# Block mask of an attention kernel: 16 more contraction rows in kept key and query buffers in place of 128 small mask products

## Chip, cores and metric

The kernel runs on one core of one Trainium2 chip. The metric is the device time of one execution in microseconds (us): the median of three runs, and beside it one execution taken by the hardware profiler, whose trace all rows below come from.

## The reference, cut to what matters

The program is one step of a two-layer streaming encoder: layer 0 has latent attention and a state-space branch side by side, layer 1 is a convolution module. Only the attention of the 2048 prompt tokens is touched here:

```
def attend(q_n, q_r, k_n, k_r, v, mask):
    s = (einsum('bqhd,bkhd->bhqk', q_n, k_n)
         + einsum('bqhr,bkr->bhqk', q_r, k_r)) * ATTN_SCALE
    s = where(mask, s, -1e30)            # key_chunk <= query_chunk, CHUNK = 64
    return einsum('bhqk,bkhd->bqhd', softmax(s), v)
```

There are 8 heads; a query or key has 64 + 32 = 96 numbers, a value 64. Queries are taken in 16 blocks of 128. Since a chunk is 64 tokens, a block needs all keys up to its own end, except that its first 64 queries must not see its last 64 keys. That corner of 64 by 64 in the last 64 key columns of each block is all that the mask does here.

## The kernel before

The program has four stages: input projections and the state-space branch (phase a), the latent attention's projections, sample attention and gating (phase b), the prompt's attention (phase c), output projection and convolution layer (phase d). All matrix products are done on pairs of a high and a low part (`h`, `l`), with three products for one: high by high, low by high, high by low.

Phase c, which the change edits, works head by head and, in a head, block by block. For block b it computes 128 by 128(b+1) scores in pieces of up to 512 keys (`chunk`): three products L1302, L1303 and L1304 over 96 rows add up in one PSUM tile `s_ps`. The last piece of a block gets a fourth product, L1306: the stationary operand `mq` is one row of 128 (64 ones, 64 zeros, bf16), the moving one `mk` one row of 64 values of -1e30, so that it adds -1e30 to the masked corner. That is 8 x 16 = 128 such products. VectorE then copies the piece to SBUF and takes the row's maximum (L1307), ScalarE does the exponential (L1318), GpSimd multiplies by the reciprocal sum (L1326), TensorE transposes (L1345), ScalarE and VectorE split the transposed piece into high and low (L1354, L1355), and TensorE multiplies by the values (L1365, L1366). `fin` adds up, gates and stores (L1374 to L1386).

The order in which these pieces are issued is written by hand: every piece gets a due time (`cum`, `LEAD`, `spread`) and the pieces are sorted by it; the tile framework then orders the instructions of each engine with a simulated timeline, so that an instruction may move ahead of others where its inputs and memory are ready. Each engine runs its own instructions in order.

`load(h)` makes new tiles `kl`, `kh`, `ql`, `qh` and `v` for a head in one of two pools, `c_kx` for even heads and `c_k` for odd ones, and issues the transfers into `kl`, `ql` and `v` (L1274 to L1278). `halves` makes the high part and leaves the low part in place: for head 0 on ScalarE and VectorE (L1286, L1287), for the others on GpSimd (L1289, L1290). A new tile takes the memory of the tile of that name two heads ago, and its first writer waits until that one has been read for the last time. `c_kx` opens at the end of phase b, whose last steps are the query rotation on GpSimd (L483 to L486), the transposes L691 and L701, the copies L692 and L702, and the reciprocal roots that begin at L671.

Of the kernel before, what the change touches and what calls it, by code (L numbers as in the profile page):

```python
# [11 lines left out]
F32R = mybir.dt.float32r  # L12
BF = mybir.dt.bfloat16
I32 = mybir.dt.int32
AF = mybir.ActivationFunctionType
OP = mybir.AluOpType
# [3 lines left out]
TP = 2048  # L20
# [16 lines left out]
def f(ap):  # L37
    return ap.bitcast(F32)
# [22 lines left out]
class K:  # L61
# [1176 lines left out]
    def phase_c(self):  # L1238
        nc, A, S = self.nc, self.A, self.S
        with ExitStack() as es:  # L1240
            cp = self.pool(es, "c_c", 1)
            sp = self.pool(es, "c_s", 2)
            kps = (self.kx, self.pool(es, "c_k", 1))
            po = self.pool(es, "c_po", 2, PSUM)
            pt = self.pool(es, "c_pt", 3, PSUM)
            ps = self.pool(es, "c_ps", 3, PSUM)
            mq = cp.tile([1, 128], BF, name="mq")
            nc.vector.memset(mq, 0.0)
            nc.vector.memset(mq[:, :64], 1.0)
            mk = cp.tile([1, 64], BF, name="mk")  # L1250
            nc.vector.memset(mk, -1e30)
            hd = {}
            cnt = [0]
            FQ, FQL = 0, 3
            PF = 0
# [4 lines left out]
            CHN = ((0, 1024, (0, 8)), (1024, 1024, (8, 16)))  # L1260

            def load(h):
                t = {}
                kp = kps[h % 2]
                for nm in "hl":
                    t["k" + nm] = kp.tile([96, TP], F32R, name="k" + nm)
                    t["q" + nm] = kp.tile([96, TP], F32R, name="q" + nm)
                t["v"] = kp.tile([128, 16, 128], F32R, name="v")
                hd[h] = t
                for c0, n, vs in CH0 if h == 0 else CH1 if h == 1 else CHN:  # L1270
                    cc = slice(c0, c0 + n)
                    dma = (nc.scalar if c0 < AQ and h == 0 else nc.sync).dma_start
                    k, q = t["kl"], t["ql"]
                    dma(f(k[:64, cc]), S["kT"][h, :, cc])  # L1274
                    dma(f(k[64:, cc]), S["krT"][:, cc])
                    dma(f(q[:, cc]), S["qT"][h, :, cc])
                    if vs:
                        dma(f(t["v"][:, vs[0]:vs[1]]), S["v"][h, :, vs[0]:vs[1]])  # L1278
                    if h == 0:
                        for nm in "kq":  # L1280
                            halves(h, nm, c0, True)

            def halves(h, nm, c0, first=False):
                hi, lo = (hd[h][nm + s][:, c0:c0 + 512] for s in "hl")
                if first:
                    nc.scalar.activation(hi, f(lo), AF.Copy)  # L1286
                    nc.vector.tensor_tensor(lo, f(lo), f(hi), op=OP.subtract)  # L1287
                else:
                    nc.gpsimd.tensor_scalar(hi, f(lo), 1.0, 1.0, op0=OP.mult, op1=OP.mult)  # L1289
                    nc.gpsimd.tensor_tensor(lo, f(lo), f(hi), op=OP.subtract)  # L1290

            def scores(h, b):
                t = hd[h]
                nk = 128 * (b + 1)
                sb = sp.tile([128, TP if nk > 1024 else 1024], F32, name="s_sb" if nk > 1024 else "s_sm", bufs=4)
                st = sp.tile([128, 16], F32, name="s_st", bufs=6)
                q = slice(b * 128, b * 128 + 128)
                items = []

                def chunk(i, k0, n, last):  # L1300
                    o = ps.tile([128, 512], F32, name="s_ps")
                    nc.tensor.matmul(o[:, :n], t["qh"][:, q], t["kh"][:, k0:k0 + n], start=True, stop=False)  # L1302
                    nc.tensor.matmul(o[:, :n], t["ql"][:, q], t["kh"][:, k0:k0 + n], start=False, stop=False)  # L1303
                    nc.tensor.matmul(o[:, :n], t["qh"][:, q], t["kl"][:, k0:k0 + n], start=False, stop=not last)  # L1304
                    if last:
                        nc.tensor.matmul(o[:, n - 64:n], mq, mk, start=False, stop=True)  # L1306
                    nc.vector.tensor_scalar(sb[:, k0:k0 + n], o[:, :n], 1.0, st[:, i - 1:i] if i else None,  # L1307
                                            op0=OP.mult, op1=OP.max, accum_out=st[:, i:i + 1])
                    if last:
                        nc.vector.tensor_scalar(st[:, 5:6], st[:, i:i + 1], -ATT, None, op0=OP.mult)  # L1310
                        e0 = 0
                        parts = []
                        while e0 < nk:
                            m = nk - e0
                            m = m if m <= 1024 else 1024 if m > 1152 else 640
                            j = 8 + len(parts)
                            parts.append(j)
                            nc.scalar.activation(sb[:, e0:e0 + m], sb[:, e0:e0 + m], AF.Exp, bias=st[:, 5:6], scale=ATT, accum_out=st[:, j:j + 1])  # L1318
                            e0 += m
                        if len(parts) == 2:  # L1320
                            nc.vector.tensor_tensor(st[:, 8:9], st[:, 8:9], st[:, 9:10], op=OP.add)
                        nc.vector.reciprocal(st[:, 7:8], st[:, 8:9])  # L1322
                        e0 = 0
                        while e0 < nk:
                            m = min(1024, nk - e0)
                            nc.gpsimd.tensor_scalar(sb[:, e0:e0 + m], sb[:, e0:e0 + m], st[:, 7:8], 1.0, op0=OP.mult, op1=OP.mult)  # L1326
                            e0 += m

                k0, i = 0, 0
                while k0 < nk:  # L1330
                    n = nk - k0
                    if n > 512:
                        n = 384 if n == 640 else 512
                    items.append((0.42 * n / 512 * 1.55, lambda i=i, k0=k0, n=n, l=k0 + n == nk: chunk(i, k0, n, l)))
                    k0 += n
                    i += 1
                return sb, items
# [116 lines left out]
            for n, (h, a, b) in enumerate(steps):  # L1454
                t0, t1 = cum[n], cum[n + 1]
                if n % 16 == 0:
                    add(cum[max(0, n - 14)] - LEAD - 4 if n else -1e9, lambda h=h: load(h))
                    if n:
                        spread(cum[n - 9] - LEAD, cum[n - 2] - LEAD, 8, lambda i, h=h: halves(h, "kq"[i % 2], 512 * (i // 2)))
                spread(t0 - LEAD - (t1 - t0), t0 - LEAD, nchunks(b), sub(("S", n), mk_s(n)))  # L1460
                spread(t0, t1, (b + 4) // 4, sub(("T", n), mk_t(n)))
                if b % 2 == 1:
                    spread(t1 + AVD, t1 + AVD + (t1 - cum[n - 1]), 2 * a + 2, sub(("A", n), mk_a(n, (n // 2) % 2, None)))
# [568 lines left out]
```

## Time and profile before

| | us |
|---|---|
| median of 3 runs | 2432.97 |
| lowest and highest of them | 2428.14, 2435.06 |
| profiled execution | 2423.48 |
| its span, first to last instruction | 2421.7 |

| engine | busy us | share of the span |
|---|---|---|
| PE (TensorE matmul) | 2251.3 | 93% |
| PEld (TensorE weight load) | 2009.7 | 83% |
| DVE (VectorE) | 1833.4 | 76% |
| ACT (ScalarE) | 1180.1 | 49% |
| POOL (GpSimd) | 1419.9 | 59% |

The weight loads overlap the matmuls; the ends of matmuls are modelled, so that two matmuls in a row overlap in the listing and the distance from one start to the next is the better measure of what one costs. The shares are averages over four stages with different limits. Attention runs from about 886 us, the first score product, to about 1407 us.

### The profile page before, as it was taken

The numbers are of one execution on the slowest core, as the hardware profiler recorded it, in microseconds if no ns is written. First come the engines' busy times: TensorE is split into PE (matmuls) and PEld (weight loads), VectorE is DVE, ScalarE is ACT, GpSimd is POOL, SyncE is SP. The second block draws the span as 40 slices with busy tenths as digits, with TensorE's granted clock in tenths as the row PEclk, the third lists the DMA queues.
The fourth block names the chain that finished last, engine by engine and source line by source line (L and its number), as shares of the span: only waits on it lengthen the run. The fifth ranks groups of instructions, "written<-read, shape, count | busy, mean of one in ns | idle before, by whom it ended". The sixth has DMA issues, their size and how long they took to land. (4 is left out here: it accounts for less than half of the span.)

```text
span 2421.7 us, 39276 instructions
## 1 busy us (share of the span) xinstructions
PE 2251.3 (93%) x13599; PEld 2009.7 (83%) x13599; DVE 1833.4 (76%) x3998; ACT 1180.1 (49%) x2226; POOL 1419.9 (59%) x1320
## 2 busy tenths in 40 slices
PE   6788989999889979999999989999999999989996
PEld 6788989996558868888888888988888889989996
DVE  7763246975447658888887855999998999999984
ACT  4343356236436657767677744433333533533423
POOL 5232543216266566667777534686768888976861
PEclk9899999999999979999999999999999999999998
DMA  9887574315727772222222356755355246434452
GB/s 190 192 228 164 136 179 146 95 49 177 235 82 221 249 235 49 61 56 67 70 71 68 96 175 217 241 179 177 105 176 173 92 131 213 148 127 138 154 166 90
DMA packets 289671, 352.10 MB, mean 145 GB/s; under 512 B 79936, under 2 KB 231808, under 8 KB 288960
## 3 DMA queue, kind: packets, MB, share of 16 engines
q1 hardware_dynamic: 288768, 348.40, 48.9%
q8 instruction: 108, 1.77, 0.3%
q10 hardware_dynamic: 704, 1.18, 0.2%
q14 instruction: 91, 0.75, 0.1%
HBM read 255.72 MB, written 93.52 MB: 144 GB/s over the span
## 5 line engine op out<-in xcount | busy, mean ns | idle before, releaser
L1655 DVE SCALAR_TENSOR_TENSOR acc<-vt,cw,acc 128x384 f32<-128x384 f32 (+2 forms) x1142 | 669.7, 659 | 2.4 <-ACT acc L1641 1.1
L1851 POOL TENSOR_TENSOR wl<-wr,wh 128x1024 fp32r<-128x1024 f32 x110 | 265.7, 2416 | 113.1 <-ACT wh L1850 111.8
L1850 ACT ACTIVATE wh<-wr 128x1024 fp32r<-128x1024 f32 x136 | 144.2, 1060 | 332.5 <-PE pp L72 173.9
L1355 DVE TENSOR_TENSOR ptl<-pt,pth 128x512 fp32r<-128x512 f32 (+2 forms) x320 | 186.1, 602 | 34.2 <-ACT pth L1354 32.9
L1354 ACT ACTIVATE pth<-pt 128x512 fp32r<-128x512 f32 (+2 forms) x320 | 161.5, 528 | 96.1 <-PE pt L1345 93.8
L71 PE MATMUL pp<-b0h,wh 128*128 128x512 f32 (+1 forms) x488 | 180.9, 371 | 6.6 <-ACT b0h L1758 6.0
L72 PE MATMUL pp<-b0l,wh 128*128 128x512 f32 (+1 forms) x488 | 180.8, 370 | 0.0
L1326 POOL TENSOR_SCALAR s_sb<-s_sb,s_st 128x1024 f32<-128x1024 f32 (+7 forms) x128 | 118.4, 938 | 105.5 <-DVE s_st L1322 47.3
L73 PE MATMUL pp<-b0h,wl 128*128 128x512 f32 (+1 forms) x488 | 180.1, 369 | 0.0
L1851 POOL TENSOR_TENSOR w<-wr,w 128x1024 fp32r<-128x1024 f32 x57 | 137.5, 2412 | 67.2 <-ACT w L1850 66.5
L71 PE MATMUL pp<-xh,vh 128*128 128x256 f32 (+1 forms) x448 | 133.8, 299 | 32.7 <-ACT vh L192 12.1
L1850 ACT ACTIVATE w<-wr 128x1024 fp32r<-128x1024 f32 x64 | 67.8, 1060 | 184.6 <-PE pp L72 113.5
L1366 PE MATMUL o<-ptl,v 128*128 128x256 f32 x576 | 151.8, 300 | 0.4 <-DVE ptl L1355 0.4
L1365 PE MATMUL o<-pth,v 128*128 128x256 f32 x576 | 149.8, 285 | 0.8 <-ACT pth L1354 0.8
L1302 PE MATMUL s_ps<-kh,qh 96*128 96x512 f32 (+3 forms) x320 | 131.8, 413 | 11.0 <-DVE s_sm L1307 6.9
L1345 PE MATMUL pt<-ident,s_sb 128*128 128x128 f32 x800 | 122.7, 279 | 12.4 <-POOL s_sb L1326 9.0
L73 PE MATMUL pp<-xh,vl 128*128 128x256 f32 (+1 forms) x448 | 132.0, 295 | 1.7 <-DVE mx L209 1.7
L71 PE MATMUL pp<-xh,wh 128*128 128x256 f32 (+1 forms) x384 | 115.0, 299 | 18.9 <-ACT qsum L230 11.3
L72 PE MATMUL pp<-xl,vh 128*128 128x256 f32 (+1 forms) x448 | 132.4, 296 | 0.0
L1318 ACT ACTIVATE s_sb<-s_sb,s_st 128x1024 f32<-128x1024 f32 (+6 forms) x128 | 122.0, 956 | 11.1 <-DVE s_st L1310 10.7
L1303 PE MATMUL s_ps<-kh,ql 96*128 96x512 f32 (+3 forms) x320 | 117.8, 368 | 0.0
L71 PEld LDWEIGHTS pp<-xh,vh 128*128 128x128 f32 x448 | 88.8, 198 | 34.4 <-ACT vh L192 12.1
(516 smaller groups left out, 7629.2 us busy)
## 6 DMA issues: line engine op xcount, KB each, us to landing
wr<-w_c SPq DMA_DIRECT2D x120, 512.0 KB, 3.5
wr<-w_o SPq DMA_DIRECT2D x80, 512.0 KB, 3.6
raw<-xT SPq DMA_DIRECT2D x28, 512.0 KB, 5.2
raw<-x SPq DMA_DIRECT2D x16, 512.0 KB, 5.5
s_v<-v_hl SPq DMA_DIRECT2D x8, 1024.0 KB, 6.1
tb<-s_x SPq DMA_DIRECT2D x32, 256.0 KB, 3.3
raw<-w_m SPq DMA_DIRECT2D x15, 512.0 KB, 6.0
v<-s_v SPq DMA_DIRECT2D x15, 512.0 KB, 5.0
```

Source lines behind the costliest of these rows:

```text
L71: mm(o, wh, xh, start=first, stop=False)
L72: mm(o, wh, xl, start=False, stop=False)
L73: return mm(o, wl, xh, start=False, stop=last)
L1302: nc.tensor.matmul(o[:, :n], t["qh"][:, q], t["kh"][:, k0:k0 + n], start=True, stop=False)
L1345: nc.tensor.transpose(p[:, i, :], sb[:, (c + i) * 128:(c + i + 1) * 128], self.ident)
L1354: nc.scalar.activation(pth[:, c:c + m, e:e + 128], p[:, :m, :], AF.Copy)
L1355: nc.vector.tensor_tensor(ptl[:, c:c + m, e:e + 128], p[:, :m, :], f(pth[:, c:c + m, e:e + 128]), op=OP.subtract)
L1365: nc.tensor.matmul(w, v[:, c, :], pth[:, c, lo:], start=c == 0, stop=False)
L1366: nc.tensor.matmul(w, v[:, c, :], ptl[:, c, lo:], start=False, stop=c == 2 * a + 1)
L1655: stt(box[i], vt[:, k:k + n], cw[:, ct, k:k + 1], src, op0=OP.mult, op1=OP.add)
L1850: act(h, r, AF.Copy)
L1851: (nc.vector if vec_split(slots[i]) else nc.gpsimd).tensor_tensor(l, r, f(h), op=OP.subtract)
```

## The change

Keys and queries get 16 more rows, one for each block. In `qh`, row 96 + b holds 1 for the first 64 queries of block b and 0 elsewhere; in `kh`, row 96 + b holds -1e30 for the last 64 keys of block b and 0 elsewhere. The high-by-high product L1302 now contracts over 112 rows and adds the mask with it; the other two keep 96 rows. To keep these rows, the four tiles of both buffers are made once, before the first head, and filled on GpSimd by eight instructions of 16 x 1024 elements that read a corner of the identity matrix. `load` takes the kept tiles in place of new ones. `mq`, `mk`, their three fills on VectorE and the product L1306 go.

```
-            mq = cp.tile([1, 128], BF, name="mq")
-            nc.vector.memset(mq, 0.0)
-            nc.vector.memset(mq[:, :64], 1.0)
-            mk = cp.tile([1, 64], BF, name="mk")
-            nc.vector.memset(mk, -1e30)
             hd = {}
+            kq = [{nm: kp.tile([112 if nm[1] == "h" else 96, TP], F32R, name=nm) for nm in ("kl", "ql", "kh", "qh")} for kp in kps]
+            eye = self.ident[96:112, 96:112][:, :, None].to_broadcast([16, 16, 64])
+            for t in kq:
+                for nm, at, val in (("kh", 1, -1e30), ("qh", 0, 1.0)):
+                    r = t[nm][96:112].rearrange("p (b e t) -> p b e t", e=2, t=64)
+                    nc.gpsimd.tensor_scalar(r[:, :, at], eye, val, 1.0, op0=OP.mult, op1=OP.mult)
+                    nc.gpsimd.tensor_scalar(r[:, :, 1 - at], eye, 0.0, 1.0, op0=OP.mult, op1=OP.mult)
...
             def load(h):
-                t = {}
+                t = dict(kq[h % 2])
                 kp = kps[h % 2]
-                for nm in "hl":
-                    t["k" + nm] = kp.tile([96, TP], F32R, name="k" + nm)
-                    t["q" + nm] = kp.tile([96, TP], F32R, name="q" + nm)
                 t["v"] = kp.tile([128, 16, 128], F32R, name="v")
...
             def halves(h, nm, c0, first=False):
-                hi, lo = (hd[h][nm + s][:, c0:c0 + 512] for s in "hl")
+                hi, lo = (hd[h][nm + s][:96, c0:c0 + 512] for s in "hl")
...
                     nc.tensor.matmul(o[:, :n], t["qh"][:, q], t["kh"][:, k0:k0 + n], start=True, stop=False)
-                    nc.tensor.matmul(o[:, :n], t["ql"][:, q], t["kh"][:, k0:k0 + n], start=False, stop=False)
-                    nc.tensor.matmul(o[:, :n], t["qh"][:, q], t["kl"][:, k0:k0 + n], start=False, stop=not last)
-                    if last:
-                        nc.tensor.matmul(o[:, n - 64:n], mq, mk, start=False, stop=True)
+                    nc.tensor.matmul(o[:, :n], t["ql"][:, q], t["kh"][:96, k0:k0 + n], start=False, stop=False)
+                    nc.tensor.matmul(o[:, :n], t["qh"][:96, q], t["kl"][:, k0:k0 + n], start=False, stop=True)
```

## Rows read from the trace of the kernel before

**Rows 1.** Stretches: us, busy (x) of PE, PEld, DVE, ACT, POOL, PE clock, DMA.

```profile
920.00:1404.00 484.00, 470.52 (x3159) 405.31 (x3158) 404.39 (x1259) 351.13 (x732) 324.21 (x341) 1.00 0.25 67
...
1380.00:1404.00 24.00, 23.31 (x147) 19.09 (x147) 22.10 (x66) 17.68 (x36) 14.09 (x16) 1.00 0.15 41
```

**Rows 2.** Waits in 920 to 1404 us: total us, times, longest.

```profile
ACT pth L1354 <- PE pt L1345: 87.3, 111, 3.5
...
PE pt L1345 <- POOL s_sb L1326: 9.0, 6, 2.9
...
DVE s_sm L1307 <- PE s_ps L1306: 5.7, 10, 1.6
```

**Rows 3.** The mask product, whole span: duration ns min/median/max, first and last start.

```profile
L1306 PEld LDWEIGHTS <-mq x128: 90/91/98, 888.0 to 1403.5; 1*128 1x128 bf16 x128
L1306 PE MATMUL s_ps<-mk,mq x128: 197/198/229, 888.0 to 1403.5; 1*128 1x64 bf16 x128
```

**Rows 4.** Matmuls in order of time: start us, duration us, line, operands, rows*columns.

```profile
1154.12 0.34 PE L1304 MATMUL s_ps<-kl,qh 96*128 96x384 f32 x1
1154.39 0.20 PE L1306 MATMUL s_ps<-mk,mq 1*128 1x64 bf16 x1
1154.52 0.50 PE L1302 MATMUL s_ps<-kh,qh 96*128 96x512 f32 x1
1154.86 0.40 PE L1303 MATMUL s_ps<-kh,ql 96*128 96x512 f32 x1
...
1155.94 0.34 PE L1303 MATMUL s_ps<-kh,ql 96*128 96x384 f32 x1
1156.12 0.34 PE L1304 MATMUL s_ps<-kl,qh 96*128 96x384 f32 x1
...
1157.46 0.60 PE L1345 MATMUL pt<-ident,s_sb 128*128 128x128 f32 x4
1157.82 0.36 PE L1366 MATMUL o<-ptl,v 128*128 128x256 f32 x1
...
1158.98 0.28 PE L1303 MATMUL s_ps<-kh,ql 96*128 96x256 f32 x1
1159.10 0.28 PE L1304 MATMUL s_ps<-kl,qh 96*128 96x256 f32 x1
...
1159.44 0.66 PE L1345 MATMUL pt<-ident,s_sb 128*128 128x128 f32 x4
1159.85 0.36 PE L1366 MATMUL o<-ptl,v 128*128 128x256 f32 x1
...
1160.41 0.28 PE L1366 MATMUL o<-ptl,v 128*128 128x256 f32 x1
1160.53 0.40 PE L1302 MATMUL s_ps<-kh,qh 96*128 96x512 f32 x1
1160.77 0.39 PE L1303 MATMUL s_ps<-kh,ql 96*128 96x512 f32 x1
```

**Rows 5.** The weight load of the product at 1154.52: start us, duration us.

```profile
1154.52 0.19 PEld L1302 LDWEIGHTS s_ps<-kh,qh 96*128 96x128 f32 x1
```

**Rows 6.** One head's stretch on full GpSimd, columns as in the first group.

```profile
1159.00:1179.00 20.00, 17.24 (x122) 14.93 (x121) 12.46 (x36) 10.45 (x22) 19.62 (x23) 1.00 0.24 72
```

**Rows 7.** The mask product in that stretch: PE busy (x), PEld busy (x), clock, DMA.

```profile
1159.00:1179.00 20.00, 0.79 (x4) 0.36 (x4) 1.00 0.24 72
```

**Rows 8.** The largest GpSimd group by shape, 880 to 1404 us: busy us, mean ns, idle before.

```profile
L1326 POOL TENSOR_SCALAR s_sb<-s_sb,s_st 128x1024 f32<-128x1024 f32 x70 | 78.6, 1126 | 104.0 <-DVE s_st L1322 47.3 <-ACT pth L1354 38.4 <-PE s_ps L1303 4.2
```

**Rows 9.** GpSimd at the end of phase b: start us, duration us, idle before.

```profile
880.09 0.29 POOL L671 TENSOR_TENSOR st<-st,e 128x48 f32<-128x48 f32 x1 [4.33 <-DVE st L661]
888.49 1.04 POOL L483 TENSOR_TENSOR q_t<-q_xr,cosTq 128x256 f32<-128x256 f32 x1 [8.11 <-DVE q_xr L476]
```

**Rows 10.** The first score products, TensorE in order of time.

```profile
886.35 0.67 PE L1302 MATMUL s_ps<-kh,qh 96*128 96x128 f32 x3 [2.66 <-ACT qh L1286]
```

**Rows 11.** What the SP queue waited for, 870 to 1410 us.

```profile
SPq L1276 <- PE s_ps L1304: 39.6, 4, 11.4
```

## The prediction, made before the change was run

> **What bounds the kernel now.** I read four views. First the stretches by engine, cut at the two ends of attention: in the 484 us from 920 to 1404, TensorE is busy 470.5 us (97%), VectorE 404.4 (84%), ScalarE 351.1 and GpSimd 324.2, at the full clock [rows 1]. The reader is to see that only one engine is nearly full there, and that the next has 80 us to spare. Second, who waits for whom in that stretch: the longest entry is ScalarE waiting for TensorE's transposes, 87.3 us in 111 waits, while TensorE's own waits for others are short, the largest 9.0 us in 6 waits for GpSimd's scaling [rows 2]. So the others follow TensorE, which runs its instructions in order. Third, TensorE's matmuls in order of time: since their durations overlap, I read each one's price as the distance from its start to the next start. Fourth, the mask product's own entry, 128 times, for the number that the change removes [rows 3].
>
> **What the mask products cost.** The product's listed 198 ns [rows 3] is not its price; the listing shows more and less than that. At 1154.12 the last real product of a piece begins, 384 columns wide; the mask product begins at 1154.39, the next block's L1302 at 1154.52 and the L1303 after it at 1154.86: 0.74 us from the first to the last of these starts [rows 4]. Without a mask, a 384-wide product takes 0.18 us to the next start (1155.94 to 1156.12) and a 512-wide L1302 0.24 (1160.53 to 1160.77), together 0.42 [rows 4]. So the mask costs 0.32 us here: it begins some 0.09 late, holds the engine 0.13, and the product behind it starts together with its own weight load (both at 1154.52 [rows 5]), so that it takes 0.34 instead of 0.24. With transposes behind it: from 1159.10 to 1159.85 0.75 us, against 0.12 for a 256-wide product (1158.98 to 1159.10) and 0.36 for four transposes (1157.46 to 1157.82), so 0.27 lost [rows 4]. Value products behind it have the same gap. 128 times 0.27 to 0.32 is 34.6 to 41.0 us; I take the middle, 38.
>
> **What the 16 rows add.** A product of 112 rows does not stand in the trace. The nearest are 96 and 128 rows: a 128-row value product 256 columns wide takes 0.12 us to the next start (1160.41 to 1160.53) and a 96-row score product of the same width 0.12 (1158.98 to 1159.10) [rows 4]. Rows show no price between them, so 112 rows cost 0; the other end is the slower rival below. L1303 and L1304 stay at 96 rows. The change from a 128-row product to the 96-row one at 1160.53 has no gap either, so changing from 112 rows to 96 and back should have none.
>
> **The eight fills on GpSimd.** The nearest rows are 1.13 us for 128 x 1024 on the same kind of instruction [rows 8] and 0.29 for 128 x 48 [rows 9]. Eight cost 2.3 to 9.0 us; each has 1024 elements in a partition, so I take the upper end. They are covered by GpSimd's idle time ahead of the attention: 4.33 us before L671 at 880.09 and 8.11 us from there to L483 at 888.49 [rows 9], 12.4 us in all. The four of the first buffer have to be done before the first score product at 886.35 [rows 10], that is 4.5 us in that gap. Queued behind a fill stand L671 and the rotation L483 to L486, for which TensorE's last transposes of phase b wait, and behind these the last keys of head 0. If one fill sits in front of L671 the start is late by about 1 us; without any cover it is late by 9.0. I take 1. The three VectorE fills of the mask operands that go are no cost now.
>
> **Kept buffers.** The transfers into `kl` and `ql` already wait for the last products of the head two before: 39.6 us in 4 waits of the SP queue [rows 11]. Behind them in that queue stand later gate loads and output stores of `fin`; TensorE waits for neither. With one kept tile the wait is for the same readers, perhaps of half a tile at a time, so between nothing and 11.4 us (the longest wait) earlier for a transfer that is issued 14 of 16 blocks ahead of its use. I take 0. `halves` moves no work and makes the same instructions on the same rows.
>
> **What of the 38 us comes through.** VectorE would be busy 404.4 of about 446 us, 91%. In 1380 to 1404 it already runs at 22.1 of 24 us, 92%, with TensorE at 97% [rows 1], so this alone does not stop the gain. One stretch in each head does: while GpSimd prepares the next head's keys it is full, 19.6 of 20 us from 1159 to 1179, and TensorE falls to 17.2 [rows 6]. Four of the head's 16 mask products lie there [rows 7] and may buy nothing, since TensorE would only wait longer for the scaled scores. If they buy nothing, 12/16 of 38, 28.5 us, remain; if all count, 38. The middle is 33, less 1 for the fills: **32 us**. What follows attention, output projection and convolution, begins when attention ends and is moved forward as a whole.
>
> The profiled execution took 2423.5 us, 1.8 more than its span; it would take 2391.5. It lies 9.5 us below the median of the runs; taking the difference off the median gives 2401 us.
>
> **A rule against it.** TensorE's matmul share may be too flattering. Judged by weight loads, TensorE has 405.3 us in the attention stretch and VectorE 404.4 [rows 1], so that neither leads. A mask product's weight load is 91 ns [rows 3], and 128 of them 11.6 us. The Trainium skill (Perfetto Trace Analysis, Identifying the Most-Contended Engine) says that matmul busy share is not a good measure because matmuls overlap, and that the share of weight loads should be used; by it the sum would be 11.6 us in place of 38. The trace here speaks for the start distances: 0.74 against 0.42 us is time in which TensorE does nothing else. But the rule is a rival.
>
> **Rivals.**
> 1. TensorE is limited by weight loads and VectorE together, and only 11.6 us come back: 2421 us. For it speak the equal sums of rows 1; against it that TensorE waits so little for others [rows 2]. Chance 0.12.
> 2. Hidden: GpSimd's full stretches and VectorE's row maxima take up what TensorE gains, or the simulated order of instructions changes for the worse, and less than 7 us remain: 2426 to 2440. For it speaks that TensorE already waits for GpSimd in each head [rows 2, 6]. Against it, GpSimd has 160 of 484 us free [rows 1]. Chance 0.09.
> 3. Slower: the weights of a 112-row product cannot be loaded ahead while products of another row count run, as those around the one-row mask product are not. Then each of the 320 L1302 products (8 heads, 4 + 8 + 12 + 16 pieces) loses what the mask product loses around itself without its own 0.13: 0.14 to 0.19 us, 45 to 61 us in all, and after the 38 saved the kernel is 7 to 23 us slower, about 2448. It decides from 38/320 = 0.12 us a product on. Against it stand the gapless changes between 128 and 96 rows [rows 4]. Chance 0.05.
> 4. More than 41 us: VectorE waits for the mask product itself, 5.7 us in 10 waits [rows 2], and if that too comes back the gain is 47, 2386 us. Chance 0.05.
>
> **How the numbers follow.** The forecast, a gain of 25 to 41 us, 2392 to 2408, has chance 0.69. This kernel's runs differ from their median by up to 5 us, and about 0.3%, 7 us, is what a measurement can tell from no change. The range takes in rival 4 at its low end, 2386 less 2 for the runs' spread, and rival 1 at its high end, 2421 with 2 more: 2384 to 2423. Outside are most of rivals 2 and 3. Faster by over 0.3%: 0.69 + 0.12 + 0.05 = 0.86; within 0.3%: 0.09, rival 2; slower: 0.05, rival 3.
>
> **What would show it.** In the new trace no one-row product; from the last L1304 of a block to the next start 0.12 to 0.24 us by width; L1302 at 112 rows with the same start distances as now (0.24 at 512 columns, where no transpose stands ahead); the attention stretch some 32 us shorter with VectorE near 91%; the stretches on full GpSimd as long as now, with longer TensorE waits for L1326. The fills would stand before 886 us, and the first score product within about 1 us of 886.35. I would be wrong if L1302's weight load began only with its product, if the fills stood between L483 and L486, or if the waits of TensorE grew by what the mask products free.

## The result and the profile after the change

| | before | after |
|---|---|---|
| median of the runs, us | 2430.55 (4 runs, 2425.19 to 2435.06) | 2409.1 (4 runs, 2402.61 to 2411.88) |
| ratio | | 0.9904 (0.9883 to 0.9926) |
| profiled execution; its span, us | 2423.48; 2421.7 | 2409.65; 2407.9 |

The change gains 21 us by the medians, 23 by the ratio (0.0096 of 2430.55); the forecast was 32 (25 to 41), and its range held gains of 10 to 49. The two profiled executions differ by 13.8 only. Executions of the same code differ by up to some 14 us ahead of attention (over the kernels of this study the 5200th matmul began between 866 and 880 us, wherever no work had been added before it), so from here on I read distances inside attention and not totals of one execution.

Engines of the kernel after over its whole span, from the page:

```profile
PE 2228.1 (93%) x13471; PEld 2006.6 (83%) x13471; DVE 1834.1 (76%) x3995; ACT 1177.0 (49%) x2226; POOL 1427.4 (59%) x1328
```

Stretches of the kernel after, columns as in [rows 1]; the third is the one that answers to [rows 6], from the first conversion of the next head's keys on:

```profile
920.00:1404.00 484.00, 463.59 (x3158) 414.71 (x3159) 422.00 (x1304) 364.35 (x766) 337.19 (x354) 0.98 0.25 68
935.00:1390.00 455.00, 438.98 (x3020) 393.33 (x3018) 403.39 (x1249) 346.54 (x730) 324.09 (x340) 1.00 0.26 70
1152.00:1172.00 20.00, 19.35 (x151) 18.10 (x150) 16.15 (x49) 14.51 (x33) 19.67 (x22) 1.00 0.17 45
```

In the middle of attention VectorE is busy 403.39 of 455 us, 89%. The stretch of [rows 6] has not gone, but it no longer holds TensorE: GpSimd is full here too, 19.67 of 20 us, and TensorE runs at 19.35, where it was at 17.2. So a full GpSimd is not by itself what TensorE waited for; the order of its work is, as the second batch shows. The waits in 920 to 1404 come next: first ScalarE's longest for TensorE, then TensorE's own, matmuls (PE) and weight loads (PEld) by themselves, those of 2.5 us and more:

```profile
ACT pth L1351 <- PE pt L1342: 65.2, 78, 2.8
PEld pt L1342 <- POOL s_sm L1323: 10.9, 12, 1.6
PEld s_ps L1301 <- DVE s_sb L1304: 8.3, 22, 1.2
PEld pt L1342 <- POOL s_sb L1323: 6.4, 8, 1.8
PE pt L1342 <- POOL s_sm L1323: 6.2, 7, 1.2
PEld s_ps L1301 <- DVE s_sm L1304: 5.3, 5, 3.6
PEld pt L1342 <- DVE ptl L1352: 5.1, 10, 0.7
PE s_ps L1301 <- DVE s_sm L1304: 4.1, 4, 3.3
PE pt L1342 <- DVE ptl L1352: 3.4, 10, 0.6
PE s_ps L1301 <- DVE s_sb L1304: 3.4, 7, 0.9
PEld o L1362 <- ACT pth L1351: 3.1, 3, 2.2
PE pt L1342 <- POOL s_sb L1323: 2.5, 2, 1.6
```

Beside [rows 2]: ScalarE waits less for TensorE (65.2 us, was 87.3), and the one kind of long wait, six times for GpSimd's scaling, has become many short ones for GpSimd and VectorE. TensorE still leads, by less.

The matmuls in order of time, in answer to [rows 4]: no product of one row is left, and a 112-row L1301 384 columns wide takes 0.18 us to the next start (1156.00 to 1156.18), a 256-wide one 0.13.

```profile
1156.00 0.34 PE L1301 MATMUL s_ps<-kh,qh 112*128 112x384 f32 x1
1156.18 0.34 PE L1302 MATMUL s_ps<-kh,ql 96*128 96x384 f32 x1
1156.36 0.34 PE L1303 MATMUL s_ps<-kl,qh 96*128 96x384 f32 x1
1156.53 0.29 PE L1301 MATMUL s_ps<-kh,qh 112*128 112x256 f32 x1
1156.66 0.28 PE L1302 MATMUL s_ps<-kh,ql 96*128 96x256 f32 x1
```

GpSimd at the end of phase b, in answer to [rows 9]: eight fills stand in front of L671, the first and the last shown, and the second L483 follows only behind head 1's halves (before, it began at 892.27, directly behind the first rotation).

```profile
880.89 1.05 POOL L1253 TENSOR_SCALAR kh<-ident 16x1024 fp32r<-16x1024 f32 x1 [0.57 <-PE pp L73]
...
888.66 1.04 POOL L1254 TENSOR_SCALAR qh<-ident 16x1024 fp32r<-16x1024 f32 x1
889.79 0.60 POOL L671 TENSOR_TENSOR st<-st,e 128x48 f32<-128x48 f32 x1
895.69 1.11 POOL L483 TENSOR_TENSOR q_t<-q_xr,cosTq 128x256 f32<-128x256 f32 x1 [5.31 <-DVE q_xr L476]
...
903.02 1.19 POOL L1288 TENSOR_SCALAR qh<-ql 96x512 fp32r<-96x512 f32 x2
904.19 0.72 POOL L483 TENSOR_TENSOR q_t<-q_xr,cosTq 128x256 f32<-128x256 f32 x1
```

TensorE at the same place, in answer to [rows 10]: the first score product, and the last transposes of phase b, which wait 7.75 us for that rotation (before, the same twelve waited 0.99 us at 895.68).

```profile
891.06 0.64 PE L1301 MATMUL s_ps<-kh,qh 112*128 112x128 f32 x3 [2.94 <-ACT qh L1285]
...
910.13 2.95 PE L701 MATMUL pt<-ident,q_n 128*96 128x128 f32 x12 [7.75 <-POOL q_n L486]
```

Counted from the same transposes of phase b (L691 x8, at 877.40 before and 881.95 after), L671 comes 5.1 us later and attention's first transposes 6.3 later.

### The profile page after: what moved, and what is told of

Read it like the earlier page. It is cut to its first block, busy times and chain, and to the rows that moved or that the text cites. A ratio compares the mean times of both kernels' runs of the same rounds, so it can differ in the third digit from the quotient of the medians.

```text
span 2407.9 us, 39063 instructions
## 1 busy us (share of the span) xinstructions
PE 2228.1 (93%) x13471; PEld 2006.6 (83%) x13471; DVE 1834.1 (76%) x3995; ACT 1177.0 (49%) x2226; POOL 1427.4 (59%) x1328
## 3 DMA queue, kind: packets, MB, share of 16 engines
q8 instruction: 107, 1.75, 0.3%
## 4 chain that ended last, share of the span: by engine, by line
PE 50%; DVE 6%; POOL 2%; ACT 2%; DMA 2%; issue 1%; SPq 0%; POOLq 0%; DVEq 0%; ACTq 0%
PE pp L71 12%; PE pp L72 12%; PE pp L73 12%; PE pt L1342 4%; PE o L1363 2%; PE o L1362 2%; PE s_ps L1301 2%; PE s_ps L1302 2%; PE s_ps L1303 2%; DVE acc L1652 1%; DVE s_sb L1304 1%; DVE ptl L1352 1%; ACT s_sb L1315 1%; DMA b1l<-s_mx_l 1%; DMA ql<-s_qT 1%
## 5 line engine op out<-in xcount | busy, mean ns | idle before, releaser
L1351 ACT ACTIVATE pth<-pt 128x512 fp32r<-128x512 f32 (+2 forms) x320 | 158.7, 527 | 67.3 <-PE pt L1342 65.2
L1301 PE MATMUL s_ps<-kh,qh 112*128 112x512 f32 (+3 forms) x320 | 131.1, 411 | 11.7 <-DVE s_sm L1304 5.2
L1302 PE MATMUL s_ps<-kh,ql 96*128 96x512 f32 (+3 forms) x320 | 118.7, 371 | 0.0
L1303 PE MATMUL s_ps<-kl,qh 96*128 96x512 f32 (+3 forms) x320 | 118.0, 369 | 0.0
```

The costliest lines, as they stand in the source:

```text
L1302: nc.tensor.matmul(o[:, :n], t["ql"][:, q], t["kh"][:96, k0:k0 + n], start=False, stop=False)
```

## The experiments

**First batch: the mask product without its replacement, both at once, and the rows brought in another way.** `x1_nomask` is the kernel before without the product (the mask is left out). `x2_bothmasks` is the changed kernel that makes the product as well. `x3_loadrows` keeps new tiles for each head, holds the 16 rows in the copies of q and of the rotary keys in memory, and loads 112 rows with each head, so that all three products run over 112 rows.

```diff
 x1_nomask, against before
-  start=False, stop=not last)
-  if last:
-      nc.tensor.matmul(o[:, n - 64:n], mq, mk, start=False, stop=True)
+  start=False, stop=True)
 x2_bothmasks, against after: the same lines, put back
 x3_loadrows, against before: x1's lines, and
-  t["k" + nm] = kp.tile([96, TP], F32R, name="k" + nm)
+  t["k" + nm] = kp.tile([112, TP], F32R, name="k" + nm)
   ("q" + nm alike; the copies in memory 16 rows longer, written in phase a)
```

> The kernel before without the mask product; the masked corner stays unmasked, so the mask is left out. No fills, no kept buffers, 96 rows. Theory A (the mask products cost 0.27 to 0.32 us each on TensorE, three quarters of it comes through, and the changed kernel gives part of it back at the end of phase b, where eight fills on GpSimd stand ahead of the add at L671): 29 to 34 us less than before, that is 6 to 12 us less than the changed kernel; steady distance between heads about 60 us as in the changed kernel. Rival B (the gain in attention is only what the changed kernel shows, 21 us, and the fills cost nothing): the same time as the changed kernel, 20 to 24 us less than before.

> The changed kernel with the mask product kept as well, so that the corner gets -1e30 twice. It has the fills, the kept buffers and the 112 rows, and no saving. Theory A: 5 to 11 us more than before, all of it at the end of phase b: the first score product and the first attention transpose late by that much, and the distance between heads as before, 63 to 64 us. Rival B: the same time as before within 0.3%. Rival C (112 rows cost something): more than 11 us over before, with a wider distance between heads.

> The 16 rows are written once to the DRAM copies of queries and rotary keys in the first 100 us of the kernel and come in with each head's transfers; all three products contract over 112 rows, halves work on 112 rows, the buffers are made anew for each head as before, and no fill stands at the end of phase b. Theory A: as fast as the kernel without a mask product, 28 to 34 us less than before, 6 to 12 less than the changed kernel. Rival B: the same time as the changed kernel. Rival C (the longer transfers, 17% more bytes, or the writes at the start cost as much as the fills): no gain over the changed kernel, with the late start in phase a.

Measured, as ratios to the kernel before on the same chip: x1 0.9933 (0.9916 to 0.9949), a gain of 16.3 us; x2 0.9998 (0.9985 to 1.0012); x3 1.0029 (1.0013 to 1.0045). So the product's absence alone brings 16 of the 23, less than either theory had for x1, and something else in the change brings as much as the fills cost, since x2, with the product, the fills and the kept buffers, stands where before stands. x3 came out as rival C: the start of the kernel is some 20 us late (its 5200th matmul begins at 894.5 us) and TensorE waits longer for GpSimd than in any other run (27.4 us at the weight loads of L1349, longest wait 8.0). The rows are to be had without kept buffers, but not at a profit in this form.

Where the other half of the product's price went in x1 is seen on TensorE between its 968 and 980 us. First the matmuls in order of time, then GpSimd's last conversion before the scaling and the scaling itself, then stretches of 2 us, columns as in [rows 1]:

```profile
968.82 0.51 PE L1343 MATMUL pt<-ident,s_sb 128*128 128x128 f32 x3
973.84 2.82 PE L1343 MATMUL pt<-ident,s_sb 128*128 128x128 f32 x12 [4.50 <-POOL s_sb L1324]
```

```profile
971.49 1.19 POOL L1289 TENSOR_SCALAR qh<-ql 96x512 fp32r<-96x512 f32 x2
972.67 2.21 POOL L1324 TENSOR_SCALAR s_sb<-s_sb,s_st 128x1024 f32<-128x1024 f32 x2
```

```profile
970.00:972.00 2.00, 0.00 (x0) 0.00 (x0) 0.82 (x2) 0.00 (x0) 2.00 (x3) 1.00 0.15 37
972.00:974.00 2.00, 0.16 (x1) 0.17 (x2) 0.00 (x0) 0.00 (x0) 2.00 (x4) 0.74 0.00 0
974.00:976.00 2.00, 2.00 (x10) 2.00 (x11) 0.38 (x1) 0.76 (x2) 2.00 (x2) 0.50 0.00 0
...
980.00:982.00 2.00, 2.00 (x21) 2.00 (x19) 1.80 (x9) 0.47 (x2) 2.00 (x3) 1.00 0.09 22
```

TensorE waits 4.5 us for a scaling that stands behind the halves on GpSimd, the granted clock falls to 0.50 (1.2 GHz) while it waits, and stays there until about 979: the next twelve transposes take 2.82 us, where twelve at the full clock took 1.75 in the kernel before (the row below). It happens once in each of six heads, with waits of 2.5 to 4.5 us (18.3 us in all). Before, the same waits are 9.0 us [rows 2]; the one of 2.85 us is followed by such a fall, those of 2.56 (this row) and 2.06 us are not.

```profile
1165.38 1.75 PE L1345 MATMUL pt<-ident,s_sb 128*128 128x128 f32 x12 [2.56 <-POOL s_sb L1326]
```

**Second batch: the kept buffers alone, and the fills.** `y1_kept` is the kernel before with buffers of 96 rows kept for all heads and the mask product as it was; `y2_kept_nomask` is that without the product (the mask is left out); `y3_kept_dma` is the changed kernel with its 16 rows brought by four transfers from a pattern in memory, in place of the eight fills.

```diff
 y1_kept, against before (y2: and x1's lines)
+  kq = [{nm: kp.tile([96, TP], F32R, name=nm) for nm in ("kl", "ql", "kh", "qh")} for kp in kps]
...
-  t = {}
+  t = dict(kq[h % 2])
-  for nm in "hl":
-      t["k" + nm] = kp.tile([96, TP], F32R, name="k" + nm)
-      t["q" + nm] = kp.tile([96, TP], F32R, name="q" + nm)
 y3_kept_dma, against after
-  nc.gpsimd.tensor_scalar(r[:, :, at], eye, val, 1.0, op0=OP.mult, op1=OP.mult)
-  nc.gpsimd.tensor_scalar(r[:, :, 1 - at], eye, 0.0, 1.0, op0=OP.mult, op1=OP.mult)
+  nc.sync.dma_start(f(kq[i][nm][96:112]), S["mrow"][j])
```

> The kernel before with kept key and query buffers of 96 rows, made once as in the changed kernel, and the mask product as it was; no fills, no 112 rows. Theory K (kept buffers let the transfers of a head begin when their part of the buffer has been read, instead of all at once after the whole tile, so that the halves on GpSimd spread over the head and TensorE no longer waits for the scaling ten us into each head; the fills then cost about 7 us at the end of phase b): 5 to 10 us less than before. Rival L (kept buffers change nothing by themselves): the same time as before within 0.3%.

> Kept buffers of 96 rows and no mask product at all (the mask is left out). It is the changed kernel without the fills and the extra rows. Theory K: 5 to 9 us less than the changed kernel, 27 to 33 us less than before, with a distance between heads of about 59 to 60 us and the first attention transpose 25 us behind the first score product, as before. Rival F (the fills cost nothing): the time of the changed kernel, 20 to 24 us less than before.

> The changed kernel, but the 16 rows of each buffer are brought by two transfers of 16 x 2048 from a DRAM pattern that is written once in the first tens of us, instead of eight fills on GpSimd at the end of phase b. Theory K: 4 to 9 us less than the changed kernel, 25 to 32 less than before. Rival F: the time of the changed kernel. Rival P (work ahead of the first transfers of phase a, or transfers ahead of the first head's keys, costs as much as the fills): no gain, with a later first score product.

Measured: y1 0.9955 (0.9936 to 0.9975), a gain of 10.9 us that the prediction had put at nothing; y2 0.9882 (0.9862 to 0.9902), 28.6; y3 0.9989 (0.9970 to 1.0008). y1 and y2 are close to what theory K says; y3 is nearest to rival P. The cause of y1's gain is in the order of GpSimd's work around the halves of one head, first the kernel before, then y1 (the copies into the high halves, eight in a head, and the scalings of two wide pieces):

```profile
1155.16 1.21 POOL L1289 TENSOR_SCALAR qh<-ql 96x512 fp32r<-96x512 f32 x2 [2.80 <-DMA ql<-s_qT]
...
1159.08 1.21 POOL L1289 TENSOR_SCALAR kh<-kl 96x512 fp32r<-96x512 f32 x2
...
1161.51 1.20 POOL L1289 TENSOR_SCALAR kh<-kl 96x512 fp32r<-96x512 f32 x2
1162.68 1.20 POOL L1289 TENSOR_SCALAR qh<-ql 96x512 fp32r<-96x512 f32 x2
...
1164.21 2.22 POOL L1326 TENSOR_SCALAR s_sb<-s_sb,s_st 128x1024 f32<-128x1024 f32 x2
```

```profile
1136.92 1.20 POOL L1287 TENSOR_SCALAR kh<-kl 96x512 fp32r<-96x512 f32 x2 [4.38 <-DMA kl<-s_krT]
...
1140.59 2.12 POOL L1324 TENSOR_SCALAR s_sb<-s_sb,s_st 128x1024 f32<-128x1024 f32 x2
1142.68 1.21 POOL L1287 TENSOR_SCALAR qh<-ql 96x512 fp32r<-96x512 f32 x2
...
1145.35 1.20 POOL L1287 TENSOR_SCALAR kh<-kl 96x512 fp32r<-96x512 f32 x2
...
1166.38 1.20 POOL L1287 TENSOR_SCALAR qh<-ql 96x512 fp32r<-96x512 f32 x2 [2.65 <-DMA ql<-s_qT]
```

With new tiles the eight copies of a head begin within 8 us: the six transfers into `kl` and `ql` are issued together, from 1150.85 to 1153.50. The scaling stands behind all of them, 9.05 us after the first. With kept tiles five transfers are issued from 1132.79 to 1138.20 and the last at 1162.26; the copies spread over 30 us, and the scaling stands behind the first two, 3.67 us after the first. GpSimd is no less full in y1 (19.75 of 20 us from 1137), but TensorE is busy 19.74 of these 20. TensorE's matmul waits for GpSimd's scaling in 920 to 1404 fall from 9.0 us [rows 2] to

```profile
PE pt L1343 <- POOL s_sb L1324: 0.6, 1, 0.6
```

y2 without the fills is 5 us below the changed kernel by the ratios (0.0022, with intervals that overlap), and from the first score to attention's first transposes it takes 25 us with no fills (24.7 to 25.8 in before, x1, x3, x4, y1, y2 and y4) and 31.3 and 32.1 with them (after, x2). So the fills cost 5 to 7 us. y3 does not win them back: the first transposes come 20.9 us after the first score, but that score itself waits for the transfer of its rows and is late; its 5200th matmul begins at 883.2, 3 us behind the latest of the kernels with nothing added before it, so that the pattern may cost something in phase a, which single executions do not show; and in attention TensorE waits 10.5 us longer than in the changed kernel (table below), mostly for VectorE. Why the latter, stays open.

**The price of the product by its shape.** `x4_mask128bf` makes the same product over 128 rows of bf16 in the kernel before (127 of them add zeros); `y4_kept_mask128r` has kept buffers and the product over 128 rows of fp32r.

```diff
 x4_mask128bf, against before
-  mq = cp.tile([1, 128], BF, name="mq")
+  mq = cp.tile([128, 128], BF, name="mq")
   (mk alike; ones in the first row alone)
 y4_kept_mask128r, against y1_kept: the same in fp32r
```

> The kernel before with the mask product widened from 1 to 128 contraction rows, 127 of them zero in the stationary operand, still bf16 and 64 columns. Theory M (the 0.3 us comes from the change of row count, one row against 96 and 128, around which no weight load runs ahead): the product costs some 0.03 to 0.1 us, weight loads run ahead of it and behind it, and the kernel gains 15 to 28 us. Rival T (it comes from the change of data type, bf16 between fp32r products): the same price of about 0.3 us and the same time as before.

> Kept buffers of 96 rows, no fills, and the mask product kept but widened to 128 rows (127 of them zero) and made of fp32r like its neighbours. Theory: in this form it costs about 0.03 to 0.08 us on TensorE instead of 0.3, so with kept buffers the kernel is within 8 us of the one without any mask product, 20 to 30 us less than before. Rival T (the price is in the row count alone and the rest stays): 0.13 us as in the bf16 form of 128 rows, about 10 to 17 us behind the kernel without a mask product.

Measured: x4 0.9963 (0.9947 to 0.9979), 9 us faster than before for a wider product, but short of theory M's 15 to 28; y4 0.9914 (0.9894 to 0.9935), 20.8, which is the changed kernel's gain with no row added to a buffer. In order of time in x4, a matmul list and then the weight loads under it:

```profile
1154.00 0.40 PE L1304 MATMUL s_ps<-kl,qh 96*128 96x512 f32 x1
1154.24 0.21 PE L1306 MATMUL s_ps<-mk,mq 128*128 128x64 bf16 x1
1154.28 0.31 PE L1302 MATMUL s_ps<-kh,qh 96*128 96x128 f32 x1
1154.42 0.28 PE L1303 MATMUL s_ps<-kh,ql 96*128 96x128 f32 x1
```

```profile
1154.24 0.10 PEld L1306 LDWEIGHTS <-mq 128*128 128x128 bf16 x1 [0.28 <-issue]
1154.24 0.20 PEld L1302 LDWEIGHTS s_ps<-kh,qh 96*128 96x128 f32 x1
```

The product holds the engine 0.04 us in place of 0.13, and starts with no gap behind L1304 (0.24 for 512 columns). What remains is that the load behind it begins only with it.

**Third batch: which engine holds the gain back.** Kept buffers in all four. `z1` and `z2` leave out GpSimd's scaling of the scores (the normalisation is left out); `z3` and `z4` leave out VectorE's low half of the probabilities, and the value products take the high half twice. z2 and z4 have no mask product (the mask is left out).

```diff
 z1 against y1, z2 against y2
-  nc.gpsimd.tensor_scalar(sb[:, e0:e0 + m], sb[:, e0:e0 + m], st[:, 7:8], 1.0, op0=OP.mult, op1=OP.mult)
 z3 against y1, z4 against y2
-  nc.vector.tensor_tensor(ptl[:, c:c + m, e:e + 128], p[:, :m, :], f(pth[:, c:c + m, e:e + 128]), op=OP.subtract)
-  nc.tensor.matmul(w, v[:, c, :], ptl[:, c, lo:], ...
+  nc.tensor.matmul(w, v[:, c, :], pth[:, c, lo:], ...
```

> Kept buffers with the mask product, and without the multiplication of the probabilities by the reciprocal sum on GpSimd (left out, so the probabilities are not normalised). It is the first of a pair. Theory G (GpSimd's full stretches hold back what the mask product frees): the pair with and without the mask product lies 30 to 40 us apart, in place of the 19 us measured with the scaling. Theory V (VectorE holds it back): the pair stays 15 to 22 us apart. This one alone: up to 10 us less than the kept buffers with scaling, by either.

> The same without the mask product (the mask and the normalisation are left out). Theory G: 30 to 40 us less than its partner with the mask product. Theory V: 15 to 22 us less.

> Kept buffers with the mask product, and without VectorE's low half of the transposed probabilities (L1355); the value products take the high half twice, so that TensorE's work is the same and VectorE loses some 190 us of about 405 in the attention stretch. First of a pair. Theory V: this pair with and without the mask product lies 30 to 40 us apart; TensorE then is the only engine near full. Theory G: it stays 15 to 22 us apart. Rival P (the mask product's price on TensorE is smaller than read from its start distances, because weight loads or issue take part of the time anyway): 15 to 22 us in both pairs.

> The same without the mask product (the mask and the low half of the probabilities are left out). Theory V: 30 to 40 us less than its partner with the mask product. Theory G and rival P: 15 to 22 us less.

Measured: z1 0.9927 (0.9911 to 0.9943), z2 0.9821 (0.9799 to 0.9843), z3 0.9899 (0.9874 to 0.9924), z4 0.9775 (0.9739 to 0.9811). The product is worth 17.7 us between y1 and y2 (0.0073 of 2424), 25.7 between z1 and z2 (0.0106), 30 between z3 and z4 (0.0124). These differences are each uncertain by some 6 to 13 us, so the runs alone do not put the three in order, nor do they exclude P, by which the product itself is cheap. The traces do: from attention's first transposes to its last value product the distance shrinks by 13.3 us from y1 to y2, 29.9 from z1 to z2 and 30.6 from z3 to z4 (table below). So P falls, and G and V are each half right: relieving either engine lets more through, one as much as the other, and neither lets all of it through.

The rest can be counted in each trace. From attention's first transposes to its last value product (which begins at 1420.0 us in the kernel before, not at about 1407 as put above) I take the distance; from it I take off the waits of TensorE's weight loads for other engines (the PEld rows of the list of waits, as those of after above, added up) and the lost clock (one minus the granted clock, added up over stretches of 5 us; it counts a little of the waits a second time):

| kernel | distance, us | waits | lost clock | what is left |
|---|---|---|---|---|
| one-row product: before | 508.5 | 24.6 | 5.0 | 478.9 |
| y1, kept buffers | 501.4 | 17.3 | 5.0 | 479.1 |
| x2, after and the product | 506.4 | 20.2 | 4.7 | 481.5 |
| z1, no scaling | 496.4 | 13.6 | 7.7 | 475.1 |
| z3, no low half | 486.7 | 4.1 | 2.9 | 479.7 |
| 128-row product: x4 | 503.1 | 34.8 | 15.3 | 453.0 |
| y4, kept buffers | 484.9 | 28.3 | 3.9 | 452.7 |
| no product: after | 484.4 | 35.5 | 7.0 | 441.9 |
| x1, new tiles | 497.5 | 39.6 | 18.8 | 439.1 |
| x3, rows loaded | 505.8 | 49.0 | 19.8 | 437.0 |
| y2, kept buffers | 488.1 | 40.3 | 7.9 | 439.9 |
| y3, rows by transfer | 495.4 | 46.0 | 4.6 | 444.8 |
| z2, no scaling | 466.5 | 24.7 | 4.3 | 437.5 |
| z4, no low half | 456.1 | 13.0 | 2.5 | 440.6 |

What is left falls into three groups, whatever else differs: 475.1 to 481.5 with the one-row product (mean 478.9), 437.0 to 444.8 without (mean 440.1), 452.9 with 128 rows. The product's price is the difference, 38.8 us, 0.30 each; over 128 rows it is 12.8, 0.10 each. And where the product goes, waits grow: y1 to y2 by 23.0 us, z1 to z2 by 11.1, z3 to z4 by 8.9.

The choice of the weight loads' waits matters. With the matmuls' own waits taken off in their place, the pairs that differ by the product alone give 31 to 36 us (y1 and y2 30.7, after and x2 31.5, z3 and z4 33.6, z1 and z2 34.7, before and x1 36.0), and the groups scatter more (446 to 469 without the product). The price is thus 31 to 39 us by the way of counting; that it is far over 11.6 holds either way.

## Why the prediction was right in its sign and high by ten

- **"What the mask products cost": right, as far as it can be told.** 38 was taken from distances between starts, 38.8 is what the table gives, inside the range of 34.6 to 41.0; counted by the matmuls' waits it is 31 to 36, at its lower end.
- **"What the 16 rows add": right.** L1301 keeps the start distances of 96 rows, and after (112 rows, 441.9) lies 2.0 us over y2 (96 rows, 439.9), x2 2.4 over y1: at most 0.01 us for each of the 320 products, and within what the table can tell. In x3 all three products run over 112 rows, and 437.0 is left.
- **"Kept buffers: I take 0": wrong, by 7 to 11 us.** I asked only when a transfer could begin. The transfers' release also sets when GpSimd gets the halves, and spread releases let the scaling through between them. The row was shown: the SP queue's 4 long waits in front of that line, 39.6 us [rows 11], are now 11, of 2.8 us in the mean for 9.9, though the longest is no shorter (the queue's waits of after in 870 to 1410):

```profile
SPq L1275 <- PE s_ps L1303: 30.5, 11, 12.5
```

- **"What of the 38 us comes through": the step that failed.** I let 28.5 to 38 through, with 4 of 16 products lost in GpSimd's full stretch. With new tiles 16.3 came through: the waits grew by 15.0 us and the lost clock by 13.8 (before to x1 in the table), and the fall of the clock behind a longer wait was in none of my terms. With kept buffers 17.7 came through, with 23.0 us more of waits and 2.9 more of lost clock: VectorE and GpSimd are close behind TensorE in many places of a head (y2's weight loads wait 17.2 us for VectorE and 19.1 for GpSimd), not only in that stretch, and that GpSimd is full there was not the cause that I took it for. "VectorE at 91% alone does not stop the gain" was too kind: with its low half gone, 30 came through. A wait list in which TensorE waits little [rows 2] tells how the engines stand now, not how much slack is behind it.
- **"The eight fills: I take 1": wrong, 5 to 7.** Each took 1.05 us, within the bound, but they stood in one block in front of L671. What I named as queued behind them, the rotation, fell behind head 1's halves, and the last transposes of phase b waited 7.75 us.
- **What would show it.** The first score came at 891.06, 4.71 late, but phase b's transposes were already 4.55 late there, so it is within 1 us of its place; it was the transposes behind it that fell back. The last fill began at 888.66 and not before 886. VectorE is at 89%, for 91. The full stretch is shorter, not as long as before (GpSimd 26.05 of 30 us from 1152, for 28.38 from 1155). TensorE's longer waits for the scaling came in x1 (18.3 us for 9.0), not in after. The last sign of being wrong, waits that grow by what is freed, came in part: 10.9 of 37.0 us from before to after, 23.0 of 39.2 from y1 to y2.

The sum as it came out, in distances inside the traces: product -37.0, waits +10.9, lost clock +2.0 (before to after in the table), start of attention +6.3; -17.8 in the two profiled executions, -21 to -23 in the runs, the rest within what single executions differ by. In edits: product -16 to -18, kept buffers -11, fills +5. Two errors of opposite sign brought the time near the forecast, and that is luck: without the 11 us of the kept buffers, put at nothing, the gain would have been 10 to 12, at the edge of the range.

On the rivals: the first gave 11.6 us by the weight loads alone, and fell, with 38.8 us off TensorE by the table and 16 to 30 coming through in the runs. The Trainium skill (Perfetto Trace Analysis, Identifying the Most-Contended Engine) names the share of weight loads as a measure of how near TensorE is to its limit; as the price of one product, which is what the prediction made of it, the weight loads' time came out too low here. Rival 2's mechanism, others taking up what TensorE gains, is real but took half, not all. Rival 3 fell with 112 rows at no price, and rival 4 with a gain of half its 47 us.

No kernel run here that masks and normalises beats the changed one clearly. y4 equals it (0.9914 against 0.9904, intervals overlapping) without fills; y2's 0.9882 shows what the change would reach if its rows cost nothing to write.

## What to carry to other kernels

An instruction's price on the leading engine and what its removal brings are two numbers: take the first from start distances, and for the second ask what every other engine's slack is, at each place, before the leader begins to wait. Replacing a tile made anew by one kept altered here when transfers were released, and with that when the work behind them landed on a shared engine; read that engine's order of work for each such edit, and not its busy share alone, and where a block of set-up work is put, read which rotation or copy falls behind the next block. Here the rare product of one row among wide ones was better made over 128 rows, with zeros; other row counts were not run.

## What the runs showed of the hardware

- **A one-row product among 96- and 128-row products costs 0.30 us, the same product over 128 rows 0.10.** The two differ in rows alone (bf16 in both before and x4; fp32r over 128 rows is no dearer, 452.7 against 453.0). Counted by the matmuls' waits the prices are 0.24 to 0.28 and 0.05 to 0.09. The Trainium skill (TensorEngine Tiling (Array Packing), Key Properties) says that a change of tiling mode drains TensorE; the gaps before and behind the one-row product (0.09 us and 0.10 at 1154.39 [rows 4]) would fit that, but the trace does not name a mode, so that this is the cause is not shown.
- **Behind waits of 2.5 to 4.5 us on TensorE the granted clock stood at half (0.50 for 1.00) for some 3 to 6 us** (six times in x1, 18.8 us of lost clock in all, against 5.0 before). Such a wait then costs more than its length. Length alone does not decide: before, waits of 2.56 and 2.06 us were followed by no fall, and in x4 one of 1.81 us was (at 1104.29).
- **GpSimd took 1.05 us for a fill of 16 x 1024 elements**, against 1.13 for 128 x 1024 on the same kind of instruction [rows 8]: an eighth of the partitions saved it next to nothing.
